# Values and keys of an RWKV scan turned by VectorE and GpSimd's transfers in place of TensorE

## The chip, the cores and the metric

One core of a Trainium2 chip runs the whole program as one launch. The metric is the device time of one execution in microseconds (us). Before the change the median of three runs is 2236.8 us (2236.69 to 2237.2). The engines are called as in the profile: PE is TensorE's matrix array and PEld its load of weights, DVE is VectorE, ACT ScalarE, POOL GpSimd, SP the engine that issues most transfers.

## The reference

One layer over 128 context tokens and 256 latent tokens (384 in all), width 2048. The input is normalised and modulated, and one projection feeds two branches: an RWKV-7 scan in both directions (32 heads of 64) and a short convolution. Both are gated, projected, merged and projected once more. The part that the change touches is the scan:

```python
def step(S, inp):
    r_t, w_t, k_t, v_t, a_t, b_t = inp
    sa = jnp.einsum('dbhij,dbhj->dbhi', S, a_t)
    S = S * w_t[..., None, :] + sa[..., :, None] * b_t[..., None, :] + v_t[..., :, None] * k_t[..., None, :]
    y = jnp.einsum('dbhij,dbhj->dbhi', S, r_t)
    return S, y
```

with `d` the two directions (the second over the reversed tokens), `v` the values, `k` the keys and `b` = the normalised key times its learning rate.

## The kernel before

All products with weights are in float32 precision made of three float32r products (`mm3`, L81 to L83): weights are split into a high part (`whi`, cast by ACT, L88) and a rest (`wlo`, subtracted by DVE, L89). A `Stream` object walks through all the projections and emits their matmuls one step of three at a time; the rest of the program calls `ds_.go(n)` to put n such steps between its own pieces. The order on PE is therefore written by hand (`manual_schedule` for PE), and PE runs exactly in it; the orders of DVE, ACT, POOL and SP are set by a scheduler, and each engine runs its own list in order.

The scan works on blocks of 128 channels (two heads), 16 blocks. Within a block the tokens are cut into six chunks of 64 (`NCH`, `C`), for two directions, so 12 chunks. For block b:

- `prep_a`, `prep_k`: decay, learning rate and normalised keys.
- `prep_b` (L672): the products `pr` (queries side) and `bk` (keys side: 64 columns of `b`, then 64 of `k`, for each chunk), both with channels on the partitions. PE forms `A` = bk' pr by chunk and head (`pA`, L708), DVE masks it into `A` (L714). Then POOL multiplies `bk` by the chunk's last decay (L721). A 32 x 32 corner of each chunk's triangular system is solved by DVE in 30 steps on 112 partitions (`ux`, `ut`, `un`, L733 and L735): the corners go from `A` to DRAM (`ui`), from there to `un` and `ux`, and the result goes back to `A` by way of `uo` (SP's transfers, L718 to L745). DVE turns the corner into `x11` (L748).
- `prep_c` (L750): `sav`, `bt`. Rows 64 to 127 of `sav` hold the values with tokens on the partitions; `bt` is `bk` with tokens on the partitions. Both come from PE's transposes (three for each direction of `v`, L774, and ten of `bk`, L783: 16 a block) and ACT's copies out of PSUM. The reversed copy of `v` is made by ACT (`vr`). Between them stand six steps of the stream (`yield 1`).
- `scan` (L795): `pav` (L861) multiplies `A` with the values, `pH` and `pX` (L853) extend the corner, POOL clears half of `A` (memset, L874), and then two chains of chunks run: `po` (L815), `pq` (L832, reads `A` and `sav`), `pu` (L839, reads `bt` and `sav`). Steps of the stream stand between all of these.
- `norm`, `finish`: the outputs of the block; `norm` has one small power on POOL (`rs`, L940).

`x11` has a tile of its own, and the two directions' `bk` are two tiles.

Of the kernel before, what the change touches and what calls it, by code (L numbers as in the profile page):

```python
# [9 lines left out]
F32 = mybir.dt.float32  # L10
F32R = mybir.dt.float32r
AF = mybir.ActivationFunctionType
ALU = mybir.AluOpType
AX = mybir.AxisListType

P = 128
D = 2048
KC = 16
T = 384
TC_ = 128  # L20
NB = 16
C = 64
NCH = 6
# [33 lines left out]
def hybrid_step(ctx, tc, cst, x_prompt, x_sample, state_f, state_b, c, c_ctx, ada_w, ada_b, norm_g,  # L57
# [3 lines left out]
    V, S, G, TE = nc.vector, nc.scalar, nc.gpsimd, nc.tensor  # L61
# [14 lines left out]
    ident = cs[:, C_ID:C_ID + P]  # L76
# [150 lines left out]
    for i in range(3):  # L227
        pr = pp.tile([P, P], F32, tag=f"prow{i}", name=f"prow{i}")
# [177 lines left out]
    r_, k_, v_, ga_ = {}, {}, {}, {}  # L406
    box = {}

    def tmp(nm):
        return box["sp"].tile([P, T], F32, tag="t", name=nm, bufs=8)  # L410
# [134 lines left out]
    sp = ctx_sc.enter_context(tc.tile_pool(name="sp", bufs=1))  # L545
# [6 lines left out]
    for i in range(3):  # L552
        t = tmp(f"lst_{i}")
# [4 lines left out]
    for m in range(4):  # L558
# [6 lines left out]
        t = tmp(f"lin_{m}")  # L565
# [3 lines left out]
        src = t[0:96, ::-1] if m % 2 else t[0:96, :]  # L569
# [12 lines left out]
    for i in range(4):  # L582
        ep = sp.tile([P, NCH, C + 1], F32, tag=f"ep{i}", name=f"ep{i}")
# [4 lines left out]
    hss = [slice(0, C), slice(C, P)]  # L588

    def bank(nm):  # L590
        return ps1.tile([P, 4, P], F32, tag="A", name=nm, bufs=5)

    def c3(a):
        return a.rearrange("p (n t) -> p n t", t=C)

    def flat(a):
        return a.rearrange("p n t -> p (n t)")
# [10 lines left out]
    un = sp.tile([112, 32, 32], F32, tag="un", name="un")  # L608
# [63 lines left out]
    def prep_b(b, o):  # L672

        r, kk = r_[b], o["kk"]
        o["pr"], o["bk"] = [], []
        for d in range(2):
            ep, em, kd, bn = o["ep"][d], o["em"][d], o["kd"][d], o["bn"][d]
            pr = sp.tile([P, NCH, P], F32, tag=f"pr{d}", name=f"pr_{b}_{d}")
            bk = sp.tile([P, NCH, P], F32, tag=f"bk{d}", name=f"bk_{b}_{d}")
            V.tensor_tensor(bk[:, :, 0:C], c3(bn[:]), c3(em[:]), ALU.mult)  # L680
            V.tensor_tensor(bk[:, :, C:P], c3(kd[:]), c3(em[:]), ALU.mult)
            V.tensor_tensor(pr[:, :, 0:C], c3(kk[:, ::-1] if d else kk[:]), ep[:, :, 0:C], ALU.mult)
            r3 = c3(r[:])
            if d == 0:
                V.tensor_tensor(pr[:, :, C:P], r3, ep[:, :, 1:C + 1], ALU.mult)
            else:
                V.tensor_tensor(pr[:, :, C:P], r3[:, ::-1, :], ep[:, :, C:0:-1], ALU.mult)
            o["pr"].append(pr)
            o["bk"].append(bk)
        yield PB0  # L690

        def blocks(A, d, e):

            es = slice(32 * e, 32 * e + 32)
            return A[es, 0, NCH * d:NCH * d + NCH, :].rearrange("s n (h t) -> s (n h) t", h=2)[:, :, es]

        ui = dp.tile([2, 2, 12, 32, 32], F32, tag="ui", name=f"ui_{b}", bufs=2)
        uo = dp.tile([2, 2, 12, 32, 32], F32, tag="uo", name=f"uo_{b}", bufs=2)

        A = sp.tile([P, 2, 2 * NCH, P], F32, tag="A", name=f"A_{b}")  # L700
        o["A"] = A
        for d in range(2):
            pr, bk = o["pr"][d], o["bk"][d]
            m0 = C_MB if d else C_MF
            pas = {(h, n0): bank(f"pA_{b}_{d}_{h}_{n0}") for n0 in (0, 4) for h in range(2)}
            for n in range(NCH):
                for h in range(2):
                    TE.matmul(pas[h, n // 4 * 4][:, n % 4, :], bk[hss[h], n, :], pr[hss[h], n, :],  # L708
                              start=True, stop=True)
            for n0, w in ((0, 4), (4, 2)):  # L710
                mk = cs[:, m0:m0 + P].rearrange("p (w t) -> p w t", t=C).unsqueeze(1).broadcast_to([P, w, 2, C])
                for h in range(2):
                    f0 = NCH * d + n0
                    V.tensor_tensor(A[:, :, f0:f0 + w, hss[h]].rearrange("p w n t -> p n w t"),  # L714
                                    pas[h, n0][:, 0:w, :].rearrange("p n (w t) -> p n w t", t=C), mk, ALU.mult)
            yield PB1
            for e in range(2):
                nc.sync.dma_start(ui[d, e].rearrange("i s t -> s i t"), blocks(A, d, e))  # L718

        for d in range(2):  # L720
            G.tensor_tensor(o["bk"][d][:], o["bk"][d][:], o["ep"][d][:, :, C:C + 1].broadcast_to([P, NCH, P]), ALU.mult)  # L721


        for g in range(2):
            nc.sync.dma_start(un[64 * g:64 * g + 48], ui[:].rearrange("d e i s t -> (d e i) s t"))
        for g in range(2):
            nc.sync.dma_start(ux[64 * g:64 * g + 48],
                              ui[:].rearrange("d e i (m g) t -> (d e i) m g t", g=2)[:, :, g, :])
        ut = sp.tile([112, 128], F32, tag="ut", name=f"ut_{b}")
        for s in range(1, 31):  # L730
            w, m = 31 - s, (s + 1) // 2
            tv = ut[:, 0:m * w].rearrange("p (a b) -> p a b", b=w)
            V.tensor_tensor(tv, ux[:, 0:m, s:s + 1].broadcast_to([112, m, w]),  # L733
                            un[:, s:s + 1, s + 1:].broadcast_to([112, m, w]), ALU.mult)
            V.tensor_tensor(ux[:, 0:m, s + 1:], ux[:, 0:m, s + 1:], tv, ALU.add)  # L735
        for g in range(2):
            dg = ux[64 * g:64 * g + 48].rearrange("p a b -> p (a b)")[:, g:512:34]
            V.tensor_scalar(dg, dg, 1.0, None, ALU.add)
            nc.sync.dma_start(uo[:].rearrange("d e i (m g) t -> (d e i) m g t", g=2)[:, :, g, :],
                              ux[64 * g:64 * g + 48])  # L740
        x11 = sp.tile([64, 24, 32], F32, tag="x11", name=f"x11_{b}")
        o["x11"] = x11
        for e in range(2):
            for d in range(2):
                nc.sync.dma_start(blocks(A, d, e), uo[d, e].rearrange("i s t -> s i t"))  # L745

        for d in range(2):
            box["turned"] = V.transpose(x11[0:32, 12 * d:12 * d + 12, :], blocks(A, d, 0)).ins  # L748

    def prep_c(b, o):  # L750

        r, v, A = r_[b], v_[b], o["A"]

        s_in = sp.tile([P, 2, C], F32, tag="s_in", name=f"s_in_{b}")
        for d in range(2):
            for h in range(2):
                for jb in range(2):
                    p0 = C * h + 32 * jb
                    nc.sync.dma_start(s_in[p0:p0 + 32, d, :].rearrange("i (b j) -> i b j", j=32),
                                      ctx_st[d][0, 0, 2 * b + h].rearrange("(b i) j -> i b j", i=32)  # L760
                                      [:, :, 32 * jb:32 * jb + 32])

        sav = sp.tile([P, 2 * NCH, P], F32, tag="sav", name=f"sav_{b}")
        bt = sp.tile([P, 2 * NCH, P], F32, tag="bt", name=f"bt_{b}")
        o["sav"], o["bkt"] = sav, bt
        for d in range(2):
            if d == 0:
                src = v
            else:
                src = tmp(f"vr_{b}")  # L770
                S.copy(src[:], v[:, ::-1])
            pv = bank(f"pv_{b}_{d}")
            for q in range(3):
                TE.transpose(pv[:, q, :], src[:, q * P:(q + 1) * P], ident)  # L774
            for e in range(2):
                S.copy(sav[C:P, NCH * d + e:NCH * d + NCH:2, :], pv[C * e:C * e + C, 0:3, :])
            yield 1
        for d in range(2):

            for n0, n1 in (((0, 4), (4, 5)), ((0, 3), (4, 6)))[d]:  # L780
                pb = bank(f"pb_{b}_{d}_{n0}")
                for n in range(n0, n1):
                    TE.transpose(pb[:, n - n0, :], o["bk"][d][:, n, :], ident)  # L783
                S.copy(bt[:, NCH * d + n0:NCH * d + n1, :], pb[:, 0:n1 - n0, :])
                yield 1
        ks = o["kd"]
        V.tensor_tensor(ks[0][:], ks[0][:], ks[1][:, ::-1], ALU.add)
        V.scalar_tensor_tensor(ks[0][:], ks[0][:], pcol(RK + b), r[:], ALU.mult, ALU.mult)
        o["bsum"] = hl_parts(ks[0], sp.tile([P, T], F32R, tag="t", name=f"bsh_{b}", bufs=8), f"bs_{b}")
        yield 1  # L790
        for h in range(2):
            for d in range(2):
                V.transpose(st[1][hss[h], d, hss[h]], s_in[hss[h], d, :])
# [178 lines left out]
    for b in range(NB):  # L972
# [10 lines left out]
        n = drive(prep_c(b, cur))  # L983
# [6 lines left out]
        w = WINDOW + (FIRST if b == 0 else LAST if b == NB - 1 else 0)  # L990
# [133 lines left out]
    for half in range(2):  # L1124
# [8 lines left out]
        for s in range(3):  # L1133
# [10 lines left out]
            if half == 1:  # L1144
                f = rsf[:, s, :]
# [37 lines left out]
```

## Time and profile before

| | |
|---|---|
| median of three runs | 2236.8 us |
| the profiled execution | 2235.6 us |
| its span, first to last instruction | 2233.8 us |
| granted clock of PE | 0.997 |
| 128x128 transposes on PE | 256, of 16020 matmuls |
| packets of transfers | 476752, 341.56 MB |
| packets of transfers that POOL issues | 1056, 0.19 MB |

The loop over the blocks runs from about 184 to 1880 us; ahead of it the modulation and the first projections, behind it the last projections. A block takes some 105 us from the third on. The page lists for each engine the time in which it was busy; for groups of instructions their line, their tiles (output, then inputs) and shapes (partitions x elements), and what ended the engine's idle time ahead of them. Times in the timeline count from the start of the span. Matmuls overlap in a pipeline, so one matmul's length is more than what it adds.

### The profile page before, as it was taken

The numbers are of one execution on the slowest core, as the hardware profiler recorded it, in microseconds if no ns is written. First come the engines' busy times: TensorE is split into PE (matmuls) and PEld (weight loads), VectorE is DVE, ScalarE is ACT, GpSimd is POOL, SyncE is SP. The second block draws the span as 40 slices with busy tenths as digits, with TensorE's granted clock in tenths as the row PEclk, the third lists the DMA queues.
The fourth block names the chain that finished last, engine by engine and source line by source line (L and its number), as shares of the span: only waits on it lengthen the run. The fifth ranks groups of instructions, "written<-read, shape, count | busy, mean of one in ns | idle before, by whom it ended". The sixth has DMA issues, their size and how long they took to land.

```text
span 2233.8 us, 40651 instructions
## 1 busy us (share of the span) xinstructions
PE 2176.1 (97%) x16020; PEld 2065.0 (92%) x16020; DVE 1491.1 (67%) x3256; ACT 1012.4 (45%) x1784; POOL 116.5 (5%) x115
## 2 busy tenths in 40 slices
PE   6999999999999999999999999999999999999998
PEld 3688999999999999999999999999999999988988
DVE  3258567787877777767778786777677775444354
ACT  4245435454545454444445454546354633333333
POOL 2000000000000000100000000000000000000000
PEclk9999999999999999999999999999999999999999
DMA  9974454445354535353444435354535474886633
GB/s 338 346 211 125 140 143 121 119 113 133 107 140 107 137 96 141 108 137 100 127 115 124 122 107 140 107 132 122 137 113 146 143 202 144 287 288 232 220 132 113
DMA packets 476752, 341.56 MB, mean 153 GB/s; under 512 B 132673, under 2 KB 458897, under 8 KB 475665
## 3 DMA queue, kind: packets, MB, share of 16 engines
q1 hardware_dynamic: 475072, 337.20, 52.6%
q8 instruction: 126, 2.06, 0.4%
q10 hardware_dynamic: 432, 1.57, 0.2%
q14 instruction: 66, 0.53, 0.1%
q0 software_dynamic: 1056, 0.19, 0.1%
HBM read 312.09 MB, written 26.21 MB: 151 GB/s over the span
## 4 chain that ended last, share of the span: by engine, by line
PE 77%; DVE 11%; DMA 5%; ACT 4%; issue 2%; SPq 1%; POOL 0%; POOLq 0%; DVEq 0%; ACTq 0%
PE d_rk L81 4%; PE d_rk L83 4%; PE d_rk L82 4%; PE d_gv L81 4%; PE d_gv L82 4%; PE d_gv L83 4%; DMA raw_adah<-in_ada_w_dram 4%; PE pA L708 2%; PE d_oa L81 2%; PE d_oa L83 2%; PE d_oa L82 2%; PE d_bc L81 2%; PE d_mb L81 2%; PE d_mb L83 2%; PE d_mb L82 2%
## 5 line engine op out<-in xcount | busy, mean ns | idle before, releaser
L81 PE MATMUL d_rk<-h_hi,whi_rk 128*128 128x384 f32 x480 | 161.9, 337 | 0.6 <-ACT lst L554 0.6
L81 PE MATMUL d_gv<-h_hi,whi_gv 128*128 128x384 f32 x480 | 161.3, 336 | 0.0
L83 PE MATMUL d_gv<-h_hi,wlo_gv 128*128 128x384 f32 x480 | 161.0, 335 | 0.0
L82 PE MATMUL d_gv<-h_lo,whi_gv 128*128 128x384 f32 x480 | 160.9, 335 | 0.0
L82 PE MATMUL d_rk<-h_lo,whi_rk 128*128 128x384 f32 x480 | 160.7, 335 | 0.0
L83 PE MATMUL d_rk<-h_hi,wlo_rk 128*128 128x384 f32 x480 | 160.7, 335 | 0.0
L733 DVE TENSOR_TENSOR ut<-ux,un 112x30 f32<-112x30 f32 (+7 forms) x480 | 119.3, 249 | 13.0
L735 DVE TENSOR_TENSOR ux<-ux,ut 112x30 f32<-112x30 f32 (+7 forms) x480 | 119.1, 248 | 12.8
L88 ACT CAST whi_gv<-raw_gv 128x1024 fp32r<-128x1024 f32 (+1 forms) x64 | 63.9, 999 | 137.3 <-PE d_rk L82 75.2
L89 DVE TENSOR_TENSOR wlo_rk<-raw_rk,whi_rk 128x1024 fp32r<-128x1024 f32 x60 | 73.2, 1223 | 66.6 <-ACT whi_rk L88 48.7
L88 ACT CAST whi_rk<-raw_rk 128x1024 fp32r<-128x1024 f32 x60 | 63.0, 1054 | 111.0 <-PE d_rk L82 34.8
L81 PE MATMUL d_bc<-h_hi,whi_bc 128*128 128x384 f32 x256 | 92.3, 361 | 0.0
L81 PE MATMUL d_bg<-h_hi,whi_bg 128*128 128x384 f32 x256 | 92.3, 360 | 0.0
L81 PE MATMUL d_gb<-h_hi,whi_gb 128*128 128x384 f32 x256 | 92.3, 360 | 0.0
L81 PE MATMUL d_bx<-h_hi,whi_bx 128*128 128x384 f32 x256 | 92.2, 360 | 0.0
L81 PE MATMUL d_ma<-h_hi,whi_ma 128*128 128x384 f32 x256 | 91.7, 358 | 0.0
L81 PEld LDWEIGHTS d_rk<-h_hi,whi_rk 128*128 128x128 f32 x480 | 90.1, 188 | 0.9 <-ACT lst L554 0.9
L81 PEld LDWEIGHTS d_gv<-h_hi,whi_gv 128*128 128x128 f32 x480 | 90.5, 189 | 0.2
L82 PEld LDWEIGHTS d_gv<-h_lo,whi_gv 128*128 128x128 f32 x480 | 90.6, 189 | 0.0
L81 PE MATMUL d_mb<-h_hi,whi_mb 128*128 128x384 f32 x256 | 90.5, 353 | 0.0
L83 PEld LDWEIGHTS d_gv<-h_hi,wlo_gv 128*128 128x128 f32 x480 | 90.4, 188 | 0.0
L82 PEld LDWEIGHTS d_rk<-h_lo,whi_rk 128*128 128x128 f32 x480 | 90.2, 188 | 0.0
(317 smaller groups left out, 6558.5 us busy)
## 6 DMA issues: line engine op xcount, KB each, us to landing
raw_adah<-in_ada_w_dram SPq DMA_DIRECT2D x64, 512.0 KB, 8.7
raw_rk<-in_w_in_dram SPq DMA_DIRECT2D x60, 512.0 KB, 5.3
raw_gv<-in_w_in_dram SPq DMA_DIRECT2D x60, 512.0 KB, 4.6
raw_ma<-in_w_in_dram SPq DMA_DIRECT2D x16, 1024.0 KB, 5.6
raw_mb<-in_w_in_dram SPq DMA_DIRECT2D x16, 1024.0 KB, 5.5
raw_bc<-in_w_in_dram SPq DMA_DIRECT2D x16, 1024.0 KB, 5.4
raw_bx<-in_w_in_dram SPq DMA_DIRECT2D x16, 1024.0 KB, 5.4
raw_bg<-in_w_in_dram SPq DMA_DIRECT2D x16, 1024.0 KB, 5.4
```

What stands on the lines that cost most here:

```text
L81: TE.matmul(out, wh, xh, start=start, stop=False)
L82: TE.matmul(out, wh, xl, start=False, stop=False)
L83: TE.matmul(out, wl, xh, start=False, stop=stop)
L88: S.copy(hi[0:rows], src)
L89: V.tensor_tensor(lo[0:rows], src, hi[0:rows].bitcast(F32), ALU.subtract)
L708: TE.matmul(pas[h, n // 4 * 4][:, n % 4, :], bk[hss[h], n, :], pr[hss[h], n, :], start=True, stop=True)
L733: V.tensor_tensor(tv, ux[:, 0:m, s:s + 1].broadcast_to([112, m, w]), un[:, s:s + 1, s + 1:].broadcast_to([112, m, w]), ALU.mult)
L735: V.tensor_tensor(ux[:, 0:m, s + 1:], ux[:, 0:m, s + 1:], tv, ALU.add)
```

## The change

The 16 transposes a block leave PE, and ACT's nine copies with them. In their place:

- DVE turns `v` (once as it is and once reversed, into a new tile `vt`) and `bk` (in place) in blocks of 32 x 32, behind the last masked `A` (`issue_after(last)`).
- POOL issues 24 transfers within SBUF, each of 32 partitions x 12 chunks x 32 elements (128 B runs): eight from `vt` to `sav`, sixteen from `bks` to `bt`. They bring each turned 32 x 32 block to the partitions of its tokens.
- The two `bk` become one tile `bks`, and `x11` becomes a part of `un`.
- The six steps of the stream that stood between the transposes stand together (`yield 6`).

```diff
@@ prep_b
-        o["pr"], o["bk"] = [], []
+        o["pr"] = []
+        bks = sp.tile([P, 2, NCH, P], F32, tag="bk", name=f"bk_{b}")
+        o["bk"] = [bks[:, d] for d in range(2)]
...
-                    V.tensor_tensor(A[:, :, f0:f0 + w, hss[h]].rearrange("p w n t -> p n w t"),
-                                    pas[h, n0][:, 0:w, :].rearrange("p n (w t) -> p n w t", t=C), mk, ALU.mult)
+                    last = V.tensor_tensor(A[:, :, f0:f0 + w, hss[h]].rearrange("p w n t -> p n w t"),
+                                           pas[h, n0][:, 0:w, :].rearrange("p n (w t) -> p n w t", t=C), mk,
+                                           ALU.mult).ins
...
         for d in range(2):
-            G.tensor_tensor(o["bk"][d][:], o["bk"][d][:], o["ep"][d][:, :, C:C + 1].broadcast_to([P, NCH, P]), ALU.mult)
+            G.tensor_tensor(bks[:, d], bks[:, d], o["ep"][d][:, :, C:C + 1].broadcast_to([P, NCH, P]), ALU.mult)
+
+        vt = sp.tile([P, 2, T], F32, tag="vt", name=f"vt_{b}")
+        with tc.issue_after(last):
+            for d in range(2):
+                V.transpose(vt[:, d], v_[b][:, ::-1] if d else v_[b][:])
+            for d in range(2):
+                V.transpose(flat(bks[:, d]), flat(bks[:, d]))
+        o["bks"], o["vt"] = bks, vt
...
-        x11 = sp.tile([64, 24, 32], F32, tag="x11", name=f"x11_{b}")
+        x11 = un[0:64, 0:24, :]
@@ prep_c
-        for d in range(2):
-            if d == 0:
-                src = v
-            else:
-                src = tmp(f"vr_{b}")
-                S.copy(src[:], v[:, ::-1])
-            pv = bank(f"pv_{b}_{d}")
-            for q in range(3):
-                TE.transpose(pv[:, q, :], src[:, q * P:(q + 1) * P], ident)
-            for e in range(2):
-                S.copy(sav[C:P, NCH * d + e:NCH * d + NCH:2, :], pv[C * e:C * e + C, 0:3, :])
-            yield 1
-        for d in range(2):
-
-            for n0, n1 in (((0, 4), (4, 5)), ((0, 3), (4, 6)))[d]:
-                pb = bank(f"pb_{b}_{d}_{n0}")
-                for n in range(n0, n1):
-                    TE.transpose(pb[:, n - n0, :], o["bk"][d][:, n, :], ident)
-                S.copy(bt[:, NCH * d + n0:NCH * d + n1, :], pb[:, 0:n1 - n0, :])
-                yield 1
+
+        x = o["vt"][:].rearrange("p d (n e t) -> p (d n) e t", e=2, t=32)
+        for e in range(2):
+            for q in range(4):
+                G.dma_start(sav[C + 32 * e:C + 32 * e + 32, :, 32 * q:32 * q + 32], x[32 * q:32 * q + 32, :, e, :])
+        x = o["bks"][:].rearrange("p d n t -> p (d n) t")
+        for p in range(4):
+            for q in range(4):
+                G.dma_start(bt[32 * p:32 * p + 32, :, 32 * q:32 * q + 32], x[32 * q:32 * q + 32, :, 32 * p:32 * p + 32])
+        yield 6
```

What the change does to the orders of POOL and DVE, in rows of the built programs: the line, the operation, output and inputs by name, and the output's shape; "x8" is eight equal rows. The numbers at the ends of names count tiles and mean nothing here.

POOL, a whole block (b = 2) before, from the products with `bk` to the next block's:

```order
L721 TENSOR_TENSOR bk_0_3848<-bk_0_3848,ep_1148 128x768
L721 TENSOR_TENSOR bk_1_3854<-bk_1_3854,ep_1150 128x768
L874 MEMSET A_3912 64x1536
L940 TENSOR_TENSOR rs_5002<-var_4999,nhalf 128x6
L721 TENSOR_TENSOR bk_0_5006<-bk_0_5006,ep_1152 128x768
```

and the same block now:

```order
L723 TENSOR_TENSOR bk_3837<-bk_3837,ep_1148 128x768
L723 TENSOR_TENSOR bk_3837<-bk_3837,ep_1150 128x768
L780 DMA sav_4084<-vt_3995 32x12x32 x8
L784 DMA bt_4085<-bk_3837 32x12x32 x16
L874 MEMSET A_3901 64x1536
L940 TENSOR_TENSOR rs_4987<-var_4984,nhalf 128x6
```

The 24 issues stand between the products and the memset that the scan's `pq` needs.

DVE, the same block, around the last masks of `A` before (`bc`, `bu` belong to the convolution branch, `wlo_rk` to the stream's next weights):

```order
L714 TENSOR_TENSOR A_3912<-pA_1_0_4_3966,cs 128x2x2x64
L714 TENSOR_TENSOR A_3912<-pA_1_1_4_3967,cs 128x2x2x64
L89 TENSOR_TENSOR wlo_rk_0_1_3944<-raw_rk_0_3936,whi_rk_0_1_3943 128x1024
L467 TENSOR_TENSOR bc_0_3760<-bc_0_3760,d_bx_0_3806 128x384
L473 SCALAR_TENSOR_TENSOR bu_0_4103<-bc_0_3760,par,bu_0_4103 128x127
```

and now:

```order
L715 TENSOR_TENSOR A_3901<-pA_1_0_4_3955,cs 128x2x2x64
L715 TENSOR_TENSOR A_3901<-pA_1_1_4_3956,cs 128x2x2x64
L728 STREAM_TRANSPOSE vt_3995<-v_3256 128x384 x2
L730 STREAM_TRANSPOSE bk_3837<-bk_3837 128x768
L89 TENSOR_TENSOR wlo_rk_0_1_3933<-raw_rk_0_3925,whi_rk_0_1_3932 128x1024
L467 TENSOR_TENSOR bc_0_3750<-bc_0_3750,d_bx_0_3796 128x384
L730 STREAM_TRANSPOSE bk_3837<-bk_3837 128x768
L473 SCALAR_TENSOR_TENSOR bu_0_4114<-bc_0_3750,par,bu_0_4114 128x127
```

Three of the four transposes come straight behind the masks, the fourth after one weight cast; all are ahead of the solve.

DVE again, between the end of the solve and the scan's first state product (`x_2` is `x11`), before:

```order
L605 TENSOR_TENSOR lo_sq_4435<-sq_4432,sqh_4434 128x384
L89 TENSOR_TENSOR lwl_2_4489<-lraw_2_4486,lwh_2_4488 96x256
L748 STREAM_TRANSPOSE x_2_4075<-A_3912 32x384 x2
L89 TENSOR_TENSOR wlo_bg_1_1_4453<-raw_bg_1_4446,whi_bg_1_1_4452 128x1024
L644 TENSOR_SCALAR kn_4525<-pn_4522 128x384
L89 TENSOR_TENSOR lwl_0_5589<-lraw_0_5586,lwh_0_5588 96x256
L866 COPY x_2_4075<-pH_4554 32x6x32 x2
```

and now:

```order
L605 TENSOR_TENSOR lo_sq_4420<-sq_4417,sqh_4419 128x384
L89 TENSOR_TENSOR lwl_2_4474<-lraw_2_4471,lwh_2_4473 96x256
L89 TENSOR_TENSOR wlo_bg_1_1_4438<-raw_bg_1_4431,whi_bg_1_1_4437 128x1024
L758 STREAM_TRANSPOSE un<-A_3901 32x384 x2
L644 TENSOR_SCALAR kn_4510<-pn_4507 128x384
L866 COPY un<-pH_4539 32x6x32 x2
```

The weight cast `wlo_bg` has moved ahead of the corner's transposes, and the cast `lwl_0` (for the next block) behind the copies.

More of the change, by code (lines that the diff above doesn't have):

```diff
@@ L678, in prep_b @@
             pr = sp.tile([P, NCH, P], F32, tag=f"pr{d}", name=f"pr_{b}_{d}")
-            bk = sp.tile([P, NCH, P], F32, tag=f"bk{d}", name=f"bk_{b}_{d}")
+            bk = o["bk"][d]
             V.tensor_tensor(bk[:, :, 0:C], c3(bn[:]), c3(em[:]), ALU.mult)
@@ L688, in prep_b @@
             o["pr"].append(pr)
-            o["bk"].append(bk)
         yield PB0
@@ L750, in prep_c @@
     def prep_c(b, o):
-        r, v, A = r_[b], v_[b], o["A"]
+        r = r_[b]
         s_in = sp.tile([P, 2, C], F32, tag="s_in", name=f"s_in_{b}")
```

## The prediction

> **What bounds the kernel now.** I read the page first, then busy time by stretch, then single stretches of the timeline. Of the page the busy row and the chain of work that ended last:
>
> ```profile
> PE 2176.1 (97%) x16020; PEld 2065.0 (92%) x16020; DVE 1491.1 (67%) x3256; ACT 1012.4 (45%) x1784; POOL 116.5 (5%) x115
> ...
> PE 77%; DVE 11%; DMA 5%; ACT 4%; issue 2%; SPq 1%; POOL 0%; POOLq 0%; DVEq 0%; ACTq 0%
> ```
>
> TensorE is busy nearly throughout and carries three quarters of the chain; GpSimd does almost nothing. The change touches only the loop over the 16 blocks, so I ask for that stretch. The row holds eight blocks of 105 us: length, then busy time and count of PE, PEld, DVE, ACT, POOL, then the clock, the DMA share and GB/s.
>
> ```profile
> 840.00:1680.00 840.00, 835.20 (x6560) 815.98 (x6560) 632.76 (x1466) 411.11 (x748) 45.58 (x32) 1.00 0.46 122
> ```
>
> PE is busy 99.4% of it at full clock; 0.6 us of idle time is left in a block. Inside the loop time is what PE has to issue, as long as nothing new makes it wait.
>
> **What goes from PE.** The rows of the two transposing lines (duration min/median/max, start of first and last):
>
> ```profile
> L774 PE MATMUL pv<-cs,v x48: 269/272/273, 195.9 to 1791.7; 128*128 128x128 f32 x48
> ...
> L774 PE MATMUL pv<-cs,vr x48: 269/272/300, 196.8 to 1794.2; 128*128 128x128 f32 x48
> ...
> L783 PE MATMUL pb<-cs,bk x160: 270/273/301, 197.6 to 1797.7; 128*128 128x128 f32 x160
> L783 PEldq EVENT_SEMAPHORE  x48: 51/51/1118, 195.1 to 1796.5; - x48
> ```
>
> 256 transposes, 16 a block. Their 272 ns is a latency in a pipeline, so the cost comes from start times. PE's timeline in the third block (b = 2), start, length, line:
>
> ```profile
> 425.57 0.49 PE L774 MATMUL pv<-cs,v 128*128 128x128 f32 x3
> ...
> 429.75 0.38 PE L783 MATMUL pb<-cs,bk 128*128 128x128 f32 x2
> ...
> 430.49 0.34 PE L81 MATMUL d_rk<-h_hi,whi_rk 128*128 128x384 f32 x1
> ...
> 438.32 0.33 PE L81 MATMUL d_rk<-h_hi,whi_rk 128*128 128x384 f32 x1
> ```
>
> From 430.49 to 438.32 only the stream runs: 15 steps of three matmuls, 7.83 us / 45 = 0.174 us each. From 425.57 to 430.49 stand all 16 transposes and 18 stream matmuls: 4.92 - 18 x 0.174 = 1.79 us for the 16. Over 16 blocks that is **28.6 us** off a PE that does not wait there. Nothing hides them, so I take all of it.
>
> **What VectorE gets.** Four transposes a block: two of 128x384, two of 128x768. Shapes that the trace has:
>
> ```profile
> L748 DVE STREAM_TRANSPOSE x<-A x32: 523/562/570, 236.9 to 1846.0; 32x384 f32<-32x384 f32 x32
> ...
> L793 DVE STREAM_TRANSPOSE st<-s_in x64: 191/230/244, 158.9 to 1768.9; 64x64 f32<-64x64 f32 x64
> ```
>
> (562 - 230) / (384 - 64) = 1.04 ns an element, so 768 take 0.56 + 384 x 1.04 = 0.96 us, and the four 2 x 0.56 + 2 x 0.96 = 3.04 us. They stand between the last masked A and the first step of the solve, which is the chain that PE's corner product pH needs at the scan's start. VectorE there, and the stretches around it (same columns as above):
>
> ```profile
> 421.99 1.95 DVE L714 TENSOR_TENSOR A<-pA,cs 128x512 f32<-128x512 f32 x4 [0.65 <-PE pA L708]
> ...
> 433.62 0.17 DVE L738 TENSOR_SCALAR ux<-ux 48x16 f32<-48x16 f32 x1 [0.19 <-DMA ux<-ui]
> ...
> 436.47 0.18 DVE L733 TENSOR_TENSOR ut<-ux,un 112x30 f32<-112x30 f32 x1
> ...
> 468.85 1.02 DVE L748 STREAM_TRANSPOSE x<-A 32x384 f32<-32x384 f32 x2 [1.12 <-DMA A<-uo]
> 469.81 1.17 DVE L89 TENSOR_TENSOR wlo_bg<-raw_bg,whi_bg 128x1024 fp32r<-128x1024 f32 x1
> ```
>
> ```profile
> 424.00:436.50 12.50, 12.50 (x79) 12.29 (x79) 7.61 (x15) 7.54 (x13) 0.07 (x1) 1.00 0.70 140
> 436.50:460.20 23.70, 23.70 (x139) 23.70 (x138) 22.11 (x74) 8.75 (x11) 0.00 (x0) 1.00 0.46 134
> ...
> sum 55.00, PE 55.00 PEld 54.14 DVE 39.70 ACT 27.37 POOL 1.45; mean PE 18.33 PEld 18.05 DVE 13.23 ACT 9.12 POOL 0.48
> ```
>
> Before the solve VectorE is idle 12.50 - 7.61 = 4.9 us: it waits for weight casts paced by PE and for ux to land at 433.6. 3.04 us fit. The transposes of bk wait for GpSimd's product with it, over at 422.59 + 1.48 = 424.07 (its row is below), before VectorE can come to them at 425.1; behind them stand weight casts whose quarter PE has not come to yet, so this wait costs nothing. The casts come 1.8 us sooner once PE is faster, so I start the solve at 435.0 to 436.5 rather than 436.47. The other end of the chain is on PE:
>
> ```profile
> 472.17 1.61 PE L861 MATMUL pav<-sav,A 64*64 64x64 f32 x48
> 473.72 0.62 PE L853 MATMUL pH<-x,A 32*32 32x32 f32 x48
> ...
> 481.13 0.61 PE L832 MATMUL pq<-sav,A 128*128 128x128 f32 x4
> ...
> 484.12 0.61 PE L839 MATMUL pu<-sav,bt 128*128 128x128 f32 x4
> ```
>
> The transposed corner is ready at 468.85 + 1.02 = 469.87, and pH wants it at 473.72: 3.85 us to spare, 2.06 when PE arrives 1.79 earlier. The weight cast wlo_bg of the last row, 1.17 us, now stands ahead of the corner's transposes on VectorE. It is paced by PE and comes sooner too; at worst it costs its 1.17 us of the 2.06, so I price it at nothing. The last block has no such room:
>
> ```profile
> 1846.00 0.56 DVE L748 STREAM_TRANSPOSE x<-A 32x384 f32<-32x384 f32 x1
> ```
>
> ```profile
> 1846.83 0.62 PE L853 MATMUL pH<-x,A 32*32 32x32 f32 x48
> ```
>
> 0.27 us: there PE will wait 1.79 - 0.27 = 1.5 us, once. I add **1.5 us**.
>
> **What GpSimd gets.** 24 transfers of 32 x 12 pieces of 128 B a block, between its two products with bk and its memset of A. Its own rows, from the start of the kernel and from blocks 0 and 2:
>
> ```profile
> 1.95 0.53 POOL L237 DMA_DIRECT2D prow<-in_mu_next_dram  x1
> 2.46 0.50 POOL L238 DMA_DIRECT2D prow<-in_norm_g_dram  x1
> ...
> 8.78 0.52 POOL L247 DMA_DIRECT2D prow<-in_mu_prev_dram  x1 [0.24 <-DMA prow<-in_k_k_dram]
> ```
>
> ```profile
> 192.87 2.38 POOL L721 TENSOR_TENSOR bk<-bk,ep 128x768 f32<-128x768 f32 x1 [4.65 <-issue]
> ...
> 422.59 1.48 POOL L721 TENSOR_TENSOR bk<-bk,ep 128x768 f32<-128x768 f32 x1 [3.37 <-PE pA L708]
> 473.91 1.38 POOL L874 MEMSET A<- 64x1536 f32 x1 [49.84 <-PE pav L861]
> ```
>
> ```profile
> m<-in_ada_b_dram POOLq DMA_DIRECT2D x16, 1.0 KB, 5.4
> ```
>
> An issue of 16 rows takes 0.50 us, one of 48 rows 0.53. Drawn on as a line, 0.03 us / 32 rows makes 0.50 + 368 x 0.00094 = 0.85 us for 384 pieces, 20 us for 24 of them. The lower end is 0.50 each, 12 us. The upper end, if the whole 0.53 us went by rows: 11 ns a piece, 4.2 us an issue, 102 us a block. I take the line, being near both rows. The row at 8.78 waits for the transfer eight issues before it, so eight are in flight; at the 5.4 us to landing of the last row, 24 take 16 us, less than the issues. The time at hand: GpSimd sits idle 49.84 us between its products and the memset. The issues can start when VectorE has turned v, about 425.1 (423.94 + 2 x 0.56); memset (1.38 us) and all must be over when PE comes to pq, 481.13 - 1.79 = 479.3. That leaves 52.8 us for 24 issues: **2.2 us each**. At 0.85 us the last one goes at about 446, and bt is first read by pu at 482. Hidden, with 30 us to spare. Behind the issues on GpSimd stand only that memset and, after the scan, the small power of the norm.
>
> **The DMA engines.** A window of 4 us in which nearly all that moves is the 128 B pieces of ui:
>
> ```profile
> DMA packets 760, 0.09 MB, mean 23 GB/s; under 512 B 760, under 2 KB 760, under 8 KB 760
> ...
> q1 hardware_dynamic: 760, 0.09, 15.4%
> ```
>
> 16 x 4 us x 15.4% / 760 = 13.0 ns a piece. The 9216 pieces of a block take 7.5 us of each engine, 7% on top of the 46% in the loop. They come while un, ux and raw_gv load: eight transfers in flight can put 8 x 384 x 13 ns / 16 = 2.5 us ahead of ux. With 0 to 2.5 us there the solve would start between 435.0 and 436.5, before or where it does now, so 2.06 us is room enough. Price zero; without that cover it is the second rival.
>
> **Smaller things.** On SP's queue lraw changes places with one weight load; lraw's cast has moved behind the scan's first copies as well, so nothing. ACT loses eight copies and vr a block; at 411 busy of 840 us it bounds nothing. pav and the first pu wait for the DMA lanes' semaphores, four waits a block more than go with pv and pb. At 51 ns each (the row of L783) that is between 0 and 3.3 us in all; the middle, **1.6 us**.
>
> **The sum**, against the profiled execution, 2235.6 us (span 2233.8 and 1.8 around it): 2235.6 - 28.6 + 1.5 + 1.6 = 2210.1. The median of the runs stands 1.2 us above that execution, so 2211 us, 1.2% less.
>
> **Rivals.**
>
> *GpSimd becomes the bound (slower).* If an issue costs by its pieces, PE waits at pq for memset and bt. It decides above 2.2 us an issue; each 0.1 us more costs 2.4 us a block, 38 us in all, so from 2.3 us the gain is gone. At the upper end of 4.2 us: 2 x 24 x 16 = 768 us, about 2975. For it: no row has a transfer of 384 pieces. Against it: three times the rows cost 6% more. Chance 0.13.
>
> *VectorE holds GpSimd's issues off (slower).* The product of block 0 took 2.38 us beside VectorE's work, 1.48 in block 2: engines do disturb each other. If issues went on only while VectorE is idle, they would have 55.0 - 39.7 - 3.0 = 12.3 us of the 55, and need 20 + 1.4: 9 us late a block, 146 in all, about 2355. Against it: scaled by 2.38 / 1.48 an issue takes 1.4 us, still under 2.2. Chance 0.07. The Trainium skill's page SBUF — State Buffer speaks against this change here: its section "A bandwidth-pool intuition that's wrong (but worth ruling out)" gives 3.1 us rather than 0.62 for a GpSimd transfer beside a VectorE copy in a two-port mode, which as an estimate would be 24 x (3.1 - 2.2) x 16 = 346 us of waiting, about 2553. But the same page, under "Who interferes with whom", has no two-port mode for tensor_tensor, which holds off only GpSimd's reads; the solve is all TENSOR_TENSOR, and the slow 2.38 us is a product that reads. So I leave that chance small.
>
> *The solve comes late (part of the gain back).* If none of the 3.04 us fits and ux lands up to 2.5 us later, pH waits up to 3.04 + 2.5 - 2.06 = 3.5 us a block, 56 us, 2266; half of that gives 2238. For it: VectorE is busy 22.11 of 23.70 us in the solve and catches nothing up. Chance 0.16, mostly under 2232.
>
> *The transposes were not on the path.* PE's room is then filled with other waits, and the time stays, 2233 to 2240. The start times speak against it. Chance 0.05.
>
> **How the numbers follow.** The forecast, 2204 to 2218, has 0.59. Up to 2241 come the late solve but for its worst (0.15), the unmoved path (0.05) and GpSimd just over its limit (0.02): 0.81 together, so the range is 2204 to 2241. About 0.2%, 4.5 us, is what a measurement can tell from no change. Faster by more: 0.59 + 0.11 of the late solve + 0.01 = 0.71. Same: 0.05 + 0.04 + 0.01 = 0.10. Slower: 0.01 of the late solve and 0.18 of GpSimd's = 0.19.
>
> **What would show it.** Right: blocks of about 103 us instead of 105, PE still over 99% busy in the loop; an issue on GpSimd of 0.5 to 1.4 us, its last one before 460 in the third block; transposes of 0.56 and 0.96 us. Wrong: PE waiting at pq or pu for GpSimd or a DMA; pH waiting for VectorE in every block; issues over 2.2 us.

## The result and the profile after

The changed kernel takes **2248.6 us** (median of five runs, 2246.2 to 2253.5), the kernel before 2236.8 us beside it. The ratio is 1.0055, with a 95% interval from 1.0042 to 1.0068: half a per cent slower. Forecast were 2211 us and a range up to 2241, so the prediction was wrong in the sign and in the range. The profiled execution took 2247.7 us, its span is 2245.6.

Of the page after, busy times, the DMA queues, the chain of work that ended last and the costliest group:

```profile
PE 2158.1 (96%) x15764; PEld 2040.9 (91%) x15764; DVE 1529.6 (68%) x3320; ACT 949.6 (42%) x1640; POOL 358.1 (16%) x499
...
q1 hardware_dynamic: 475072, 337.20, 55.7%
q0 software_dynamic: 13344, 19.08, 5.1%
...
PE 16%; DVE 2%; DMA 2%; issue 1%; ACT 0%; SPq 0%; POOL 0%; POOLq 0%; DVEq 0%; ACTq 0%
...
L784 POOL DMA_DIRECT2D bt<-bk x256 | 157.2, 617 | 95.8 <-DMA sav<-vt 42.2
```

and SP's queue on the page before:

```profile
q1 hardware_dynamic: 475072, 337.20, 52.6%
```

PE has its 256 matmuls less and is busy 18 us less, yet the span grew. GpSimd issues a transfer in 0.617 us. Its queue (q0) takes 5.1% of 2245.6 us, 7.2 us of every DMA engine in a block. The same 475072 packets of SP's queue (q1) took 52.6% of 2233.8 us before and take 55.7% of 2245.6 us now, 76 us more of each engine. The chain can't be set against that of before: its shares add up to 21%, so it breaks off after the loop. The busy time of eight blocks, in the stretch that was shown of before (length, PE, PEld, DVE, ACT, POOL, clock, DMA share, GB/s):

```profile
840.00:1680.00 840.00, 819.74 (x6373) 796.43 (x6372) 645.84 (x1488) 377.51 (x673) 164.96 (x223) 1.00 0.57 132
```

PE idles 20.3 us there instead of 4.8. What it waited for between 200 and 1860 us before (total, times, longest), the whole list:

```profile
PE po L815 <- DVE st L844: 7.6, 9, 1.6
PE pv L774 <- DVE A L714: 1.4, 1, 1.4
PE d_ob L82 <- DVE ybl L509: 1.3, 2, 1.0
PE pu L839 <- ACT sav L834: 1.3, 6, 0.2
PE pq L832 <- DVE sav L816: 0.9, 2, 0.4
```

and of the list now the rows that are new:

```profile
PE pl L83 <- DVE lwl L89: 5.9, 11, 0.5
PE d_bx L81 <- DVE ga L440: 4.1, 3, 2.0
PE d_ma L81 <- DVE ga L440: 3.2, 2, 2.5
PE pH L853 <- issue: 3.1, 1, 3.1
PE d_bg L81 <- DVE ga L440: 3.0, 3, 1.3
PE d_bc L81 <- DVE ga L440: 2.9, 2, 1.5
...
PE pH L853 <- DVE un L758: 1.1, 4, 0.5
```

No row has PE wait for GpSimd or for a transfer. It waits for VectorE: for `ga`, which frees an accumulator bank of the stream, and for `lwl`, a rest of weights. In VectorE's list both stand behind the solve. (The 3.1 us at `pH` are one wait in the last block; "issue" means that the profile shows no releaser for it.) Why the solve is late shows in VectorE's timeline of the third block (b = 2):

```profile
416.74 1.95 DVE L715 TENSOR_TENSOR A<-pA,cs 128x512 f32<-128x512 f32 x4 [0.77 <-PE pA L709]
418.61 1.03 DVE L728 STREAM_TRANSPOSE vt<-v 128x384 f32<-128x384 f32 x2
419.56 0.94 DVE L730 STREAM_TRANSPOSE bk<-bk 128x768 f32<-128x768 f32 x1
...
431.40 0.18 DVE L748 TENSOR_SCALAR ux<-ux 48x16 f32<-48x16 f32 x1 [1.93 <-DMA ux<-ui]
432.29 0.19 DVE L743 TENSOR_TENSOR ut<-ux,un 112x30 f32<-112x30 f32 x1 [0.71 <-DMA ux<-ui]
...
437.78 1.23 DVE L89 TENSOR_TENSOR wlo_gv<-raw_gv,whi_gv 128x1024 fp32r<-128x1024 f32 x1 [2.24 <-ACT whi_gv L88]
...
458.34 0.19 DVE L745 TENSOR_TENSOR ux<-ux,ut 112x15 f32<-112x15 f32 x1
...
459.57 0.55 DVE L440 TENSOR_TENSOR ga<-ga,d_gv 128x384 f32<-128x384 f32 x1
...
467.41 1.06 DVE L758 STREAM_TRANSPOSE un<-A 32x384 f32<-32x384 f32 x2 [2.72 <-DMA A<-uo]
```

The last masked `A` is over at 418.7 and the turns by 423. Then VectorE waits for `ux`, starts the solve at 432.3 and stands still within it at 437.8, at a weight cast whose `whi_gv` ACT has not made. ACT, in turn, waited for the load, as its row shows, and the whole run's waits and landings (the last number is the median us from issue to landing) repeat it:

```profile
436.70 2.00 ACT L88 CAST whi_gv<-raw_gv 128x1024 fp32r<-128x1024 f32 x2 [8.48 <-DMA raw_gv<-in_w_in_dram]
```

```profile
ACT whi_gv L88 <- DMA raw_gv<-in_w_in_dram: 149.4, 21, 10.3
...
DVE ux L748 <- DMA ux<-ui: 40.6, 16, 6.0
```

```profile
raw_gv<-in_w_in_dram SPq DMA_DIRECT2D x60, 512.0 KB, 10.4
```

and the same row before:

```profile
raw_gv<-in_w_in_dram SPq DMA_DIRECT2D x60, 512.0 KB, 4.6
```

A load of `raw_gv` landed 4.6 us after its issue before. Now it takes 10.4. The transfers that delay it, from GpSimd's timeline of the same block, run all through the time in which `un`, `ux` and `raw_gv` load (SP issues those from 421.6 to 430):

```profile
420.23 4.95 POOL L780 DMA_DIRECT2D sav<-vt  x8 [1.40 <-ACT whi_rk L88]
...
441.73 0.62 POOL L784 DMA_DIRECT2D bt<-bk  x1 [0.98 <-issue]
468.47 1.38 POOL L874 MEMSET A<- 64x1536 f32 x1 [26.12 <-PE pav L861]
```

GpSimd then sits idle for 26 us. And PE's row of the corner product:

```profile
468.33 0.62 PE L853 MATMUL pH<-un,A 32*32 32x32 f32 x48
```

The corner was 3.85 us ahead of `pH` in this block before; now its turn ends at 468.47, as `pH` begins. In numbers for the whole loop: counted from the end of the last masked `A`, as means over the third to the fifteenth block, the solve started at 12.5 us, lasted 23.9 (to the end of its last step) and the corner was turned at 46.0 before; now it starts at 14.1, lasts 27.0 and the corner is turned at 50.6. A block takes 106.0 us instead of 104.9 (from `pav` to `pav`). The same four numbers follow for every experiment; a block's own can be read off the rows above: 432.29 - 418.69 = 13.6, 458.53 - 432.29 = 26.2 and 468.47 - 418.69 = 49.8.

### The profile page after: what moved, and what is told of

Same layout as the page of the kernel before. It is cut to its first block, busy times and chain, and to the rows that moved or that the text cites. A ratio compares the mean times of both kernels' runs of the same rounds, so it can differ in the third digit from the quotient of the medians.

```text
span 2245.6 us, 40717 instructions
## 1 busy us (share of the span) xinstructions
PE 2158.1 (96%) x15764; PEld 2040.9 (91%) x15764; DVE 1529.6 (68%) x3320; ACT 949.6 (42%) x1640; POOL 358.1 (16%) x499
## 3 DMA queue, kind: packets, MB, share of 16 engines
q1 hardware_dynamic: 475072, 337.20, 55.7%
## 5 line engine op out<-in xcount | busy, mean ns | idle before, releaser
L784 POOL DMA_DIRECT2D bt<-bk x256 | 157.2, 617 | 95.8 <-DMA sav<-vt 42.2
L940 POOL TENSOR_TENSOR rs<-var,nhalf 128x6 f32<-128x6 f32 x16 | 21.6, 1351 | 680.5 <-DVE var L938 680.5
L89 DVE TENSOR_TENSOR wlo_gv<-raw_gv,whi_gv 128x1024 fp32r<-128x1024 f32 (+1 forms) x64 | 73.9, 1154 | 35.7 <-ACT whi_gv L88 29.3
L874 POOL MEMSET A<- 64x1536 f32 x16 | 22.0, 1376 | 462.6 <-PE pav L861 409.0
L81 PE MATMUL d_ob<-ybh,whi_ob 128*128 128x384 f32 x256 | 88.9, 347 | 3.0 <-DVE smb L521 2.1
## 6 DMA issues: line engine op xcount, KB each, us to landing
raw_gv<-in_w_in_dram SPq DMA_DIRECT2D x60, 512.0 KB, 10.4
```

The lines of the kernel that those rows point to most:

```text
L81: TE.matmul(out, wh, xh, start=start, stop=False)
L89: V.tensor_tensor(lo[0:rows], src, hi[0:rows].bitcast(F32), ALU.subtract)
L784: G.dma_start(bt[32 * p:32 * p + 32, :, 32 * q:32 * q + 32], x[32 * q:32 * q + 32, :, 32 * p:32 * p + 32])
L874: G.memset(A[C:P, 0, :, :], 0.0)
L940: G.tensor_tensor(rs[:], var[:], nhalf[:], ALU.pow)
```

## The experiments

The theory at the start was that the transfers' traffic makes the loads land late, and with them the solve. Its rivals were that VectorE's turns make it late, and that nothing is gained by taking transposes off PE.

**Is it the transfers or the turns?** Four kernels. The first leaves out the 24 transfers:

```diff
-                G.dma_start(sav[C + 32 * e:C + 32 * e + 32, :, 32 * q:32 * q + 32], x[32 * q:32 * q + 32, :, e, :])
-                G.dma_start(bt[32 * p:32 * p + 32, :, 32 * q:32 * q + 32], x[32 * q:32 * q + 32, :, 32 * p:32 * p + 32])
+        if b == 0: G.memset(sav[:], 0.0); G.memset(bt[:], 0.0)
```

> The changed kernel with its 24 transfers a block left out: sav and bt are cleared once and never get values or keys (so that part of the scan is not computed); VectorE still turns v and bk, PE does no transposes. If the transfers' traffic is what costs (it keeps the DMA engines from the loads of raw_gv, un and ux, so the solve on VectorE ends late): 2206 to 2214 us. If VectorE's four turns are what costs: 2235 to 2249 us, as with the transfers.

Measured: 2211.3 us, ratio 0.9887 (0.987 to 0.9903). Without the transfers the forecast's gain is there in full, turns and all: blocks of 103.1 us. Next, the transposes back on PE, no turns, and 24 transfers of the same shape into a tile that nobody reads:

```diff
+            G.dma_start(dm[32 * p:32 * p + 32, q % 2], x[32 * q:32 * q + 32, :, 32 * p:32 * p + 32])
...
+                TE.transpose(pv[:, q, :], src[:, q * P:(q + 1) * P], ident)
+                    TE.transpose(pb[:, n - n0, :], o["bk"][d][:, n, :], ident)
```

> PE's 16 transposes and ACT's copies back, no turns on VectorE, but 24 transfers of the same shape a block, from bk to a tile that nobody reads. Traffic theory: the 36 to 40 us that the changed kernel lost come on top of the kernel before, 2265 to 2280 us. Turns theory: nobody waits for these transfers, 2235 to 2242 us.

Measured: 2244.5 us, ratio 1.0037 (1.0022 to 1.0052), outside both ranges. In its profiled execution (2251.1 us) the solve starts at 14.6 and the corner is turned at 49.2, 3.2 us later than before. But in the kernel before, with its transposes, PE comes to `pH` at 49.8, so most of that is still covered: a kernel with more work on PE has more room for a late solve. The turns left out, the transfers kept:

```diff
-                V.transpose(vt[:, d], v_[b][:, ::-1] if d else v_[b][:])
-                V.transpose(flat(bks[:, d]), flat(bks[:, d]))
```

> The changed kernel without VectorE's four turns: the transfers carry bk as it is and a cleared vt (values and keys reach the scan unturned, so its result is not the reference's). Traffic theory: 2240 to 2250 us, nearly as the changed kernel. Turns theory: 2207 to 2216 us.

Measured: 2251.9 us, ratio 1.0065 (1.0048 to 1.0081), just above the traffic theory's range. The solve starts no sooner (14.9), the block takes 105.7. The transfers, which need not wait for turns here, also start sooner; but turns without transfers cost nothing, and transfers without turns cost as much as both. The turns are not the cause. Last, all 24 issues kept, with a twelfth of the bytes:

```diff
-sav[C + 32 * e:C + 32 * e + 32, :, 32 * q:32 * q + 32], x[32 * q:32 * q + 32, :, e, :]
+sav[C + 32 * e:C + 32 * e + 32, 0:1, 32 * q:32 * q + 32], x[32 * q:32 * q + 32, 0:1, e, :]
```

> The changed kernel, with all 24 issues at their place, but each moves one chunk instead of twelve (32 pieces of 128 B, a twelfth of the bytes); sav and bt are cleared once, so eleven twelfths of the values and keys are left out of the scan. Theory traffic: 2207 to 2216. Rival, the issues themselves or their semaphores cost (GpSimd's descriptor work beside VectorE, lanes): 2235 to 2252.

Measured: 2209.9 us, ratio 0.9881 (0.9865 to 0.9898). The issues (0.50 us each here instead of 0.62) and their semaphores cost nothing; what they move does. Bytes and pieces of 128 B were cut alike, so this run does not tell which of the two counts.

**When do the bytes cost?** The transfers are made to wait for a step s of the solve, by a flag that VectorE sets and GpSimd copies:

```diff
+            if s == 9:
+                with tc.issue_after(st_): V.memset(flag[:], 0.0)
+                o["held"] = G.tensor_copy(seen[:], flag[:]).ins
...
+                with tc.issue_after(o["held"]):
                     G.dma_start(...)
```

> The changed kernel, its 24 transfers held back until the ninth step of the solve (GpSimd reads a flag that VectorE writes there), behind the loads of un, ux and raw_gv. Traffic theory: ux and raw_gv land as before the change, most of the 28.6 us comes out, 2208 to 2222 us; sav and bt are there in time. Turns theory: no change against the changed kernel, 2244 to 2252 us; if the transfers are now late for pav or pu, slower than that.

Measured: 2211.9 us, ratio 0.9889 (0.9874 to 0.9904). By now the theory had two forms: A, the loads ahead of the solve being late is what costs; B, `raw_gv` being late inside it costs as well. The same with `s == 1`:

> The changed kernel, with the 24 transfers held until VectorE has done the first step of the solve; un and ux have landed by then, but the last two loads of raw_gv (issued 426 to 430 in the third block) and the casts that stand inside the solve come after. Correct output. Theory A, the loads ahead of the solve (un, ux) being late is what costs: 2208 to 2216, as with the hold at step 9. Theory B, raw_gv late inside the solve costs as well: 2222 to 2245. In both, GpSimd's last issue of the third block is over by 450, so the scan is not kept waiting.

Measured: **2208.1 us**, ratio 0.9874 (0.9859 to 0.9889), the fastest of all. Its rows (SP's queue and a median landing, then the stretch of eight blocks):

```profile
q1 hardware_dynamic: 475072, 337.20, 53.3%
...
raw_gv<-in_w_in_dram SPq DMA_DIRECT2D x60, 512.0 KB, 5.0
```

```profile
840.00:1680.00 840.00, 835.30 (x6518) 818.04 (x6517) 659.87 (x1534) 387.72 (x684) 177.31 (x249) 1.00 0.55 137
```

PE is busy 99.4% again, in blocks of 103.1 us. This speaks against theory B only in so far as it was put: `raw_gv` was hardly late here, since most of it had landed. With `s == 30`, the last step:

> The changed kernel, with the 24 transfers held until VectorE has done the last step of the solve (about 456 in the third block); then eight transfers of sav have 9 us until pav (465) reads them, and 24 issues of 0.62 us plus the memset of A (1.4 us) take until about 473, just ahead of pq at 474.5; bt's last lands about 477, where pu reads it. Correct output. Traffic theory: no load of the solve is touched, but the solve's way back to A (uo, A<-uo, landing about 462) now shares the DMA engines: 2212 to 2240, the time above 2212 being waits of PE at pH, pq or pu. If instead the place did not matter and the transfers always cost the same: 2245 to 2255.

Measured: 2349.9 us, ratio 1.0509 (1.0486 to 1.0532), a miss far above both. The solve is as early as with the hold to step 1 (start 11.2), but PE is kept waiting within the scan (these rows add up to 92.4 us):

```profile
PE pu L847 <- ACT sav L842: 32.0, 13, 3.1
PE po L823 <- DVE st L850: 25.5, 14, 2.4
PE pav L869 <- DMA bt<-bk: 14.3, 5, 4.1
PE pav L869 <- DMA sav<-vt: 12.7, 12, 3.9
PE pq L840 <- POOL A L882: 7.9, 4, 3.1
```

In the third block the issues took from 460.7 to 484.3, not the 15 us expected: in between, GpSimd waits for earlier transfers to land, as it did in the change, where the 24 took from 420.2 to 442.4. The memset of `A` came after them. The way back of the corner was slowed as well (turned at 50.7). So there is a window, and step 30 is past its end. Only `bt` held until step 9, `sav` at once:

```diff
+        with tc.issue_after(s8):
+            o["held"] = G.tensor_copy(seen[:], flag[:]).ins
...
+                with tc.issue_after(o["held"]):
                     G.dma_start(bt[...], ...)
```

> The changed kernel, with the eight transfers to sav issued at once (as in the change) and the sixteen to bt held until step 9 of the solve. A third of the traffic, 2.4 us of each DMA engine, meets un, ux and the first raw_gv. Correct output. If the dose counts (lateness in proportion to the traffic): 2208 to 2222, because the 1.9 us of room left by the faster PE take up most of it. If the first transfers are what costs (they stand ahead of un and ux): 2235 to 2252.

Measured: 2209.6 us, ratio 0.9879 (0.9865 to 0.9894). Its waits beside `ux` and `raw_gv`:

```profile
ACT whi_gv L88 <- DMA raw_gv<-in_w_in_dram: 39.1, 6, 7.3
DVE ux L754 <- DMA ux<-ui: 31.4, 16, 3.6
```

This is the run that ended theory A: `ux` keeps VectorE for 31.4 us in all (40.6 in the change, 4.2 with the hold to step 1) and the solve starts at 13.8, nearly as late as in the change, yet nothing is lost, because the solve runs through in 24.3 us and the corner is turned at 47.5. So I tried the other half: the transfers put off by memsets of a scratch tile on GpSimd, three, six or nine of them, behind a flag that VectorE sets once `v` is turned.

```diff
+        for i in range(6):
+            with tc.issue_after(o["held"]):
+                o["held"] = G.memset(scr[:], 0.0).ins
```

> The changed kernel, with three memsets of a scratch tile on GpSimd ahead of the 24 transfers (about 0.9 us each by the 1.38 us of 64x1536): the first issue of the third block goes at about 423.3 instead of 420.2. Correct output. Theory A, un and ux late ahead of the solve is what costs: ux (issued 423.2 to 424.7) still lands behind up to eight transfers, so 2235 to 2252. Theory B, raw_gv late inside the solve is what costs (issued 424.7 to 430): 2235 to 2252 too. This is the curve's first point: A and B agree.

Measured: 2246.7 us, ratio 1.0044 (1.003 to 1.0059). Start 13.3, length 27.5, corner 50.2, block 105.7: nearly as in the change. It lies in both ranges.

> The changed kernel, with six such memsets ahead of the transfers: first issue at about 426, when un and ux are on their way (undisturbed they land by 428.7) and three of the four raw_gv loads are not. Correct output. Theory A: 2208 to 2218. Theory B: 2222 to 2248, with VectorE idle inside the solve for 2.5 us or more a block, as in the change, and ux landing within 5 us.

Measured: 2212.8 us, ratio 0.9889 (0.9871 to 0.9907), inside theory A's range. But the trace does not bear theory A out:

```profile
ACT whi_gv L88 <- DMA raw_gv<-in_w_in_dram: 69.1, 18, 6.7
...
DVE wlo_gv L89 <- ACT whi_gv L88: 27.6, 29, 2.8
```

`raw_gv` is late, the casts inside the solve wait for it in total as long as in the change (27.6 us, there 28.8), and the solve lasts 27.1 us, as long as in the change. It starts at 11.3, though, and the corner is turned at 47.8. That still costs nothing.

> The changed kernel, with nine such memsets ahead of the transfers: first issue at about 428.8, behind un and ux and three of the raw_gv loads; only the last load (issued at 430) meets the traffic, and its weights are wanted late in the solve. Correct output. Theory A: 2207 to 2213. Theory B: 2208 to 2225, between the run before it and the hold at step 1 (2208).

Measured: 2209.5 us, ratio 0.9869 (0.9854 to 0.9884), in both ranges; corner at 47.2. (The first issue of the third block went at 431.1, later than expected and nearly as with the hold to step 1.) Neither half of the lateness costs by itself: not the late start alone (only `sav` early), not the stretched solve alone (six memsets). What they have in common is a limit: without its transposes PE comes to `pH` at 47.9 to 48.0 in every run in which it hardly waits. Corners at 46.3 to 47.8 are free, those at 50.1 and later are paid for.

**Does a late solve alone cost it?** The kernel held until step 1, with n transposes of a scratch tile between the first two steps of the solve. No load is touched.

```diff
+            if s == 2:
+                z = st_
+                for i in range(n):
+                    with tc.issue_after(z): z = V.transpose(scr[:], scr[:]).ins
```

With n = 5:

> The kernel with the transfers held until the first step of the solve (2208), with five transposes of a scratch tile (128x768, 0.94 us each) put into VectorE's list between the first and the second step of the solve: the solve ends up to 4.7 us later, some of it taken up by waits for weight casts that it had before, and no load is touched. Correct output. Theory, the end of the solve is what sets the block once it is more than about 1.6 us later than in that kernel, whatever made it late: 2235 to 2255, with TensorE waiting at the same places as in the change (pl, the stream's banks behind ga, pH). Rival, the transfers' traffic costs TensorE in another way and a late solve is only a companion: 2207 to 2220.

Measured: 2330.7 us, ratio 1.0423 (1.0405 to 1.044), above both: other work of VectorE moved up between the steps, and the corner came 8.5 us later (54.9) rather than 4.7. `ga` is among what moved up, so PE does not pay at the banks, as the theory had it, but nearly all at `pH`, 73.6 us, and some at `lwl`. Two smaller doses were to cover the change's own size, n = 2 and n = 4:

> As the run with five extra transposes between the first two steps of the solve, but with two (1.9 us). Correct output. The corner is turned 1.9 to 2.5 us later than with the transfers held (46.4 us behind the last mask of A there), so 48.3 to 48.9, and TensorE comes to pH at 48.0. Theory, only what goes beyond TensorE's arrival costs, at the rate of the other runs (1.1 to 1.3 us of block for 1 us): 2212 to 2230. Rival, a late solve costs nothing by itself: 2206 to 2211.

> The same with four extra transposes (3.8 us) between the first two steps of the solve. Correct output. The corner comes 3.8 to 6.5 us later than with the transfers held, 50.2 to 52.9 us behind the last mask of A, as in the change (50.6) or later. Theory: blocks of 105.6 to 109 us, 2245 to 2300. Rival: 2206 to 2215.

Measured: 2211.8 us (ratio 0.9892, 0.9876 to 0.9909) with two, just under the theory's range, since the corner came at 47.0 and not at 48.3; and 2310.8 us (1.0336, 1.0321 to 1.0352) with four, corner at 53.6, a little above it. PE's waits with four:

```profile
PE pH L869 <- issue: 56.1, 13, 5.3
```

A late solve by itself has a price, and below PE's arrival it has none. The size at the change's own corner, 50.6, is not shown by these runs: with four transposes the corner came later than that, with two sooner. All of them in one table (us; start, length, corner and block as above):

| run | time | start | length | corner | block |
|---|---|---|---|---|---|
| before | 2236.8 | 12.5 | 23.9 | 46.0 | 104.9 |
| the change | 2248.6 | 14.1 | 27.0 | 50.6 | 106.0 |
| no transfers | 2211.3 | 11.0 | 25.4 | 46.3 | 103.1 |
| a twelfth of the bytes | 2209.9 | 11.3 | 25.1 | 46.4 | 103.1 |
| held to step 1 | 2208.1 | 11.1 | 25.3 | 46.4 | 103.1 |
| held to step 9 | 2211.9 | 11.2 | 25.3 | 46.9 | 103.1 |
| two extra transposes | 2211.8 | 11.1 | 28.2 | 47.0 | 103.1 |
| nine memsets | 2209.5 | 11.2 | 26.5 | 47.2 | 103.1 |
| only `sav` early | 2209.6 | 13.8 | 24.3 | 47.5 | 103.2 |
| six memsets | 2212.8 | 11.3 | 27.1 | 47.8 | 103.3 |
| no turns | 2251.9 | 14.9 | 24.9 | 50.1 | 105.7 |
| three memsets | 2246.7 | 13.3 | 27.5 | 50.2 | 105.7 |
| four extra transposes | 2310.8 | 11.1 | 32.9 | 53.6 | 110.4 |
| five extra transposes | 2330.7 | 11.2 | 33.8 | 54.9 | 111.9 |

(The dummy transfers and the hold to step 30 have another path and are left out.)

The gap between corners at 47.8 and 50.1 closes block by block. The runs of the table without PE's transposes have 156 blocks (third to fourteenth). Their length is taken here from the end of one block's last masked `A` to the next one's:

| corner turned at (us) | blocks | mean length (us) |
|---|---|---|
| below 48 | 86 | 103.1 |
| 48 to 49 | 12 | 103.6 |
| 49 to 50 | 13 | 105.2 |
| 50 to 51 | 13 | 106.0 |
| 51 to 52 | 6 | 106.7 |
| 52 to 53 | 4 | 108.8 |
| above 53 | 22 | 111.2 |

Up to PE's arrival the length stays, behind it the length grows with the corner. The blocks from 48 to 52 us are all of runs with early or held transfers, those above 53 all of runs with extra transposes.

## Why the prediction was wrong, by its own steps

- **What bounds the kernel, and 28.6 us off PE: right.** With the traffic out of the way the sum of 2210.1 us stands: 2211.3 without the transfers, 2208.1 with them held. Blocks of 103.1 us were forecast as "about 103".
- **The turns fit VectorE's idle time: right.** 0.94 us and 1.03 us for a pair, instead of 0.96 and 1.12, and taking them out changes nothing for the better.
- **GpSimd's issues: right in their cost.** 0.617 us each, inside the bounds and under the limit of 2.2 us. The last went 23.0 us behind the last masked `A` (441.73 - 418.69), forecast about 22 (446 - 423.9). That nearness is luck: the forecast had 20 us of issuing and held the landings to take less, while 14.8 of the 22.1 us were issuing and the rest waits for earlier transfers, which landed 6.0 to 7.2 us after their issue (medians of `sav` and `bt`) and not 5.4. The rival that made GpSimd the bound fell: 384 pieces take 0.617 us where 16 rows took 0.50. VectorE did not hold it off either. The 3.1 us of the Trainium skill's page SBUF — State Buffer (section "A bandwidth-pool intuition that's wrong (but worth ruling out)") did not appear in the 256 issues of `bt`, which took 0.617 to 0.627 us.
- **The size of the traffic: right.** 7.2 us of each DMA engine a block, forecast 7.5.
- **"Price zero" for the DMA engines: this step failed.** It put one load, `ux`, behind eight transfers and set 2.5 us against 2.06 us of room. That part came out near: the solve starts 3.0 us later than with the transfers held (14.1 against 11.1; the forecast 435.0 to 436.5 is 11.1 to 12.5 us behind the mask), the room is 1.5 us there (47.9 - 46.4), and a lateness of `ux` alone is indeed free: with only `sav` early the solve starts at 13.8 and the corner comes at 47.5, because a solve that starts late waits less for casts inside it. The step left out what loads after `ux`. The transfers run all through the loads of `raw_gv`, whose casts stand inside the solve on an engine that runs in order, so the solve is also stretched, to 27.0 us from 25.3. Start and stretch together bring the corner 4.2 us later; 2.7 us of it lie beyond PE's arrival, and blocks of 106.0 instead of 103.1 us follow.
- **The rival that happened was "the solve comes late".** It was given 0.16, and its worst, 3.5 us a block, is near the 2.9 measured; but more than half of it was put down to the turns, which cost nothing, so that is luck. Its place was wrong in part: PE pays mostly at the stream's banks (`ga`) and at `lwl`, which stand behind the solve in VectorE's list, and less at `pH`. Of the 2.9 us a block, (20.3 - 4.7) / 8 = 2.0 are idle time of PE. Set beside the run held to step 1, matmul by matmul (third to fourteenth block), the starts give the whole: 1.9 us at the six products of the stream that wait for `ga`, 0.6 at `pl`, which waits for `lwl`, 0.2 at `pH` and 0.2 at `d_gv`. The idle time shows less than that because a stream matmul counts as busy for some 0.33 us where the next can start after 0.17, so the first part of a wait is not counted.
- **The last block's 1.5 us** is there (3.1 us at `pH` in the change, 1.2 when held, 2.8 without transfers). The 1.6 us for semaphores are too small for these runs to tell.

## What to carry to other kernels

Transfers that replace work of a compute engine have a price by the time at which they run: list every load that is in flight then, and for each the first instruction in an in-order list that needs it, not only the load that the next step waits for. Put such transfers where nothing urgent loads: here a flag from the first step of the solve turned 0.5% slower into 1.3% faster. And the room on the critical chain shrinks by what is taken off the bounding engine, so lateness that was free before is not free after.

## What the hardware showed beside this

A wait of PE can cost more than its length, because the clock is halved for a while behind it. With five extra transposes, PE waited 5.5 us at `pH` in the third block; its timeline, and the stretches around it with the granted clock ahead of the DMA share:

```profile
473.37 0.95 PE L869 MATMUL pH<-un,A 32*32 32x32 f32 x48 [5.48 <-issue]
...
475.06 0.52 PE L83 MATMUL d_bg<-h_hi,wlo_bg 128*128 128x384 f32 x1
475.38 0.52 PE L81 MATMUL d_bg<-h_hi,whi_bg 128*128 128x384 f32 x1
```

```profile
474.00:478.00 4.00, 4.00 (x37) 3.94 (x30) 1.20 (x4) 2.51 (x6) 0.00 (x0) 0.50 0.08 25
478.00:482.00 4.00, 4.00 (x67) 3.71 (x67) 2.42 (x4) 1.78 (x4) 0.00 (x0) 0.93 0.02 4
```

From 473.4 to about 478.5 PE works at a clock of 0.50, matmuls start every 0.32 us instead of 0.17, and some 2.5 us are lost again. That is enough for the 1.8 us by which the cost of a block there (8.8 us) exceeds the 7.0 us beyond PE's arrival (54.9 - 47.9). The Trainium skill's page TensorE: Matmul & The Clock Gate (section "What's actually happening") has half the clock after an idle window of about 3.4 us. The trace agrees for the long waits: behind each of the 26 at `pH` with four and five extra transposes, 3.5 to 7.1 us, the clock is 0.50. But in the change it is halved behind shorter ones as well, of 1.73 us (779.3) and of 2.53 us (1520.5):

```profile
1520.53 0.69 PE L81 MATMUL d_ma<-h_hi,whi_ma 128*128 128x384 f32 x1 [2.53 <-DVE ga L440]
```

```profile
1520.30:1523.70 3.40, 3.17 (x10) 3.17 (x11) 3.40 (x8) 0.00 (x0) 0.00 (x0) 0.50 0.95 285
```

and not behind others of 1.95 us (566.3) and 1.81 us (1627.2). So no wait of 3.4 us is needed for it, and a wait's length alone did not decide. The 1.00 of the change's eight blocks is a mean that rounds such a stretch of 3.4 us away.

The 24 transfers and SP's loads share the same DMA engines whoever issues them: the 475072 packets of SP's queue take 76 us more of each engine beside early transfers. Beside held ones they take 53.3% of 2204.8 us, 1175 us, which is what they took before (52.6% of 2233.8 us): the larger share is only the shorter span. The Trainium skill's page DMA: Bandwidth & Descriptors says in "Issuing engines are not separate DMA queues" that transfers of all engines run on the same 16 and interleave, and the row of q1 beside early transfers agrees.
